# The second block of a two-model kernel in another order, with VectorE and ScalarE in written order

## The chip, the cores and the metric

The kernel runs on one core of a Trainium2 chip. The metric is device time in microseconds (us), the median of several executions. Before the change it is 2164.07 us, the median of 3 runs from 2163.93 to 2165.48. The engines are TensorE (PE; its weight loads are PEld), VectorE (DVE), ScalarE (ACT), GpSimd (POOL) and SyncE (SP), which issues the loads of weights.

## The reference, cut to what matters

256 tokens of width 1024 in float32 go through a first model (two layers, each with a mixer and a product-key expert stage) and then through a second block. The change lies in the mixer half of the second block:

```python
def second_block(x, ...):
    h = rmsnorm(x, ln1_g)                    # x: the first model's normed output
    z = h @ w_in                             # 1024 -> pool 256, mLSTM q,k 512, v 256, o 256, i,f 8, attention q,k,v 1536
    po = pool_mixer(z[pool], pool_w, pool_scale)
    qk = silu(causal_dwconv(z[mq,mk], m_conv))         # 4 taps
    mo = sigmoid(z[o]); mi, mf = z[i] + b_i, z[f] + b_f
    hm = mlstm(qk, z[v], mi, mf)                       # log-sigmoid, cumulative sum, running maximum
    hm = rmsnorm(hm, m_norm_g) * mo
    aq, ak = rmsnorm(z[q], a_q_g), rmsnorm(z[k], a_k_g)   # per head, 8 heads of 64
    ao = moba_attention(aq, ak, z[av])                 # causal softmax within the 256 tokens
    x = x + concat([po, hm, ao]) @ w_out
    ...                                                # norm, gated FF with a 3-tap conv, unchanged
```

Two norms meet at its start: the first model's last norm (gain `gbc`) gives the residual stream, and `ln1` the input of `w_in`. The kernel computes both scales at once from x and from y = x * gbc.

## The kernel before, in words

**Units of weights.** All matrices stream from memory once, in pieces of 128 x 1024 float32 (512 KB) that are called units; `units` fixes their order, and SP loads them in that order, up to four ahead. Each unit is split into two reduced-precision parts, so that three products give float32 accuracy: ScalarE rounds the raw unit into `wh` (line 127) and VectorE or GpSimd subtracts it for `wl` (line 128, by the letters of `lo_on["pat"]`). There are four raw buffers and three of `wh` and `wl`; `prepare()` issues the split of the unit three ahead, so the high part waits until TensorE has done the unit just used.

**Two kinds of products.** `c_unit` (lines 159 to 161) gives 128 channels by 256 tokens: 24 matmuls of 256 columns into one bank. `t_mm` (lines 177 to 181) takes the activations as columns of 512: 12 matmuls into banks 4 to 7, which stay occupied over all units of a token-major product. The eight PSUM banks are called `bank_92` to `bank_99` in the built program, that is banks 0 to 7.

**Start of the block.** The expert stage ends in banks 4 to 7. `landing` adds these to x (line 245 in the last stage) and transposes x by 128 x 128 into banks 0 to 3; `settle` turns the transposes into `xh` (ScalarE, line 278) and `xl` (VectorE, line 279), 16 of each. `norm_scales_final` takes sums of squares on ScalarE and makes two inverse roots with one Newton step each; `spread` makes two diagonal matrices in `gt` (line 328) and lets TensorE spread the scale over all partitions into `rbc`, by which the channel-major results are multiplied.

**The 31 units of `block2`.** In this order: 8 token-major units `tm` (mLSTM v and o, attention v), one unit for the gates (`gw`), 4 for the mLSTM's q and k (`mqk`), 8 for the attention's q and k (`aqk`), 2 for pooling (`pin`), and 8 of the output product (`wo`). Between them stand `gates` (32 rows by 256 tokens, with Abs, Exp and Ln on ScalarE and two scans on VectorE), `conv4` (four taps on VectorE and a Silu each), `ml_*` (the mLSTM), and `at_*` (attention by pairs of heads: normalise, scores, softmax, transpose, values).

**What sets the order.** TensorE's and SP's instructions stand in the order in which they are written. VectorE's, ScalarE's and GpSimd's are ordered by a scheduler, and `behind()` and `keep_in_program_order` hold single ones back. In the block, low parts go to GpSimd from the gates to the fourth output unit (`lo_on["pat"] = "P"`), and by a pattern before.

Of the kernel before, what the change touches and what calls it, by code (L numbers as in the profile page):

```python
# [40 lines left out]
def kernel(ctx: ExitStack, tc: tile.TileContext, a, out):  # L41
# [43 lines left out]

    units = []
    for nm in a["order"]:
        w = a[nm]
        units += [w[i] for i in range(w.shape[0])]
# [82 lines left out]
    def t_mm(h, l, sh, sl, first, last):  # L172
        for b in range(2):
            bs = slice(b * 128, b * 128 + 128)
# [97 lines left out]
    def settle(g, low=False, dst=None):  # L272

        h, l = dst or (xh, xl)
        for b in range(2):
# [26 lines left out]
    def norm_scales_final(gbc):  # L302


        y = ar(120, 8).rearrange("p (b d) -> p b d", b=2)
        q = 32
        for b in range(2):
            for n in range(2):
                ns = slice(n * 512, n * 512 + 512)
                P.tensor_tensor(y[:, b, ns], x[:, b, ns], gbc[:, ns], op=ALU.mult)  # L310
                with behind(st["after"]):
                    sumsq(b, n)
                    sumsq(b, n, y, q)
            V.tensor_scalar(col(b, 2), col(b, 0), 1.0 / 1024, EPS, op0=ALU.mult, op1=ALU.add)
            V.tensor_scalar(col(b, 7), col(b, 0, q), 1.0 / 1024, None, op0=ALU.mult)
            V.tensor_scalar(col(b, 4), col(b, 1), 1.0 / 1024, col(b, 2), op0=ALU.mult, op1=ALU.add)
            V.tensor_scalar(col(b, 2, q), col(b, 4), EPS, col(b, 7), op0=ALU.mult, op1=ALU.add)
            S.activation(col(b, 3, q), col(b, 1, q), AF.Sqrt, bias=col(b, 2, q), scale=1.0 / 1024)
            V.tensor_scalar(col(b, 4, q), col(b, 1, q), 1.0 / 1024, col(b, 2, q), op0=ALU.mult, op1=ALU.add)
            root(b, q)  # L320
            S.activation(col(b, 3), col(b, 4), AF.Sqrt)
            root(b)
            V.tensor_scalar(x[:, b], y[:, b], col(b, 5), None, op0=ALU.mult)

    def spread(bk, off=0):

        for b in range(2):
            V.tensor_scalar(gt[b][:, :128], ident, col(b, 5, off), None, op0=ALU.mult)
            T.matmul(bk[:, b * 128:b * 128 + 128], ones, gt[b][:, :128], start=True, stop=True)
        V.tensor_copy(rbc, bk[:, :256])  # L330
# [19 lines left out]
    V.tensor_tensor(sm[:, 48:56], cols[:, C_FNG:C_FNG + 8], cols[:, C_LN1:C_LN1 + 8], op=ALU.mult)  # L350

# [483 lines left out]
    def block2():  # L835
        sg = ar(64, 2).rearrange("p (b n) -> p b n", b=2)
        settle(g2, low=True)

        for k in range(8):
            h, l = unit()  # L840
            t_mm(h, l, xh[:, k], xl[:, k], k == 0, k == 7)
            prepare()
            if k == 0:
                norm_scales_final(gbc)
        for b in range(2):
            r = col(b, 5, 32)
            S.activation(vau[:, b, :, 0:64], bank[4 + b * 2][:, 0:256].rearrange("p (h e) -> p h e", h=4),
                         AF.Copy, scale=r)
            S.activation(sg[:, b], bank[4 + b * 2][:, 256:512], AF.Sigmoid, scale=r)
            S.activation(tok[:, b, 512:1024], bank[5 + b * 2], AF.Copy, scale=r)  # L850
        spread(bank[3], 32)
        V.memset(vau[:, :, :, 64:65], 1.0)
        table("natural_log_exp_and_others")
# [8 lines left out]
        V.memset(onz, 1.0)  # L862

        def gates():
            V.tensor_tensor(g64, bank[2][0:64, :256], rbc[0:64], op=ALU.mult)
            V.tensor_scalar(g64, g64, cols[0:64, C_MBI:C_MBI + 1], None, op0=ALU.add)
            f = g64[32:64]
            S.activation(lf[:, 0], f, AF.Abs)
            S.activation(lf[:, 0], lf[:, 0], AF.Exp, scale=-1.0)
            V.tensor_scalar(lf[:, 1], lf[:, 0], 1.0, None, op0=ALU.add)  # L870
            S.activation(lf[:, 2], lf[:, 1], AF.Ln)
            V.tensor_scalar(lf[:, 3], lf[:, 1], -1.0, None, op0=ALU.add)
            V.tensor_tensor(lf[:, 0], lf[:, 0], lf[:, 3], op=ALU.subtract)
            last = S.activation(lf[:, 1], lf[:, 2], AF.Exp, scale=-1.0)
            V.tensor_tensor(lf[:, 0], lf[:, 0], lf[:, 1], op=ALU.mult)
            V.tensor_tensor(lf[:, 0], lf[:, 0], lf[:, 2], op=ALU.add)
            V.tensor_scalar(lf[:, 1], f, 0.0, None, op0=ALU.min)
            V.tensor_tensor(gc, lf[:, 1], lf[:, 0], op=ALU.subtract)
            V.tensor_tensor_scan(gc, onz[0:32], gc, 0.0, op0=ALU.mult, op1=ALU.add)
            V.tensor_tensor(R[0:32], g64[0:32], gc, op=ALU.subtract)  # L880
            V.tensor_tensor_scan(mx, onz[0:32], R[0:32], 0.0, op0=ALU.mult, op1=ALU.max)
# [462 lines left out]
```

## Time and profile before

| | |
|---|---|
| median of 3 runs | 2164.07 us |
| profiled execution, its own time | 2165.04 us |
| its span / mean granted TensorE clock | 2162.9 us / 0.994 |
| TensorE busy | 2123.0 us (98%) |
| VectorE / ScalarE / GpSimd busy | 1598.8 / 1141.7 / 223.4 us |
| second block's mixer half on TensorE | from 1830.28 to about 1965.5 us |

Busy times are of one execution. A matmul's end is modelled, so a busy TensorE is not TensorE at its peak; the granted clock (PEclk) tells how fast its clock was, with 1.00 for 2.4 GHz and 0.50 for 1.2 GHz. Idle time counts where the engine that bounds the stretch waits.

### The profile page before, as it was taken

Reading aid. Unit: us, or ns where it says so; the run is one execution under the profiler, and the core shown is the slowest. Engines: PE = TensorE matmul, PEld = TensorE weight load, DVE = VectorE, ACT = ScalarE, POOL = GpSimd, SP = SyncE. Lnnn points to the kernel's source line nnn. Section 1 sums busy time; section 2 is a strip of 40 time slices with the busy share of each in tenths; the row PEclk is TensorE's granted clock in tenths of the full one; section 3 lists DMA queues with packets and bytes.
Section 4 is the critical chain, followed back from the end, with each engine's and each line's share of the span. In section 5 each row is a group of like instructions: output and inputs, shape, how many; then the busy total and the mean of one; then the engine's idle time right before and its main releaser. Section 6 shows DMA issues by size and latency. Waiting matters only on the chain.

```text
span 2162.9 us, 38249 instructions
## 1 busy us (share of the span) xinstructions
PE 2123.0 (98%) x14590; PEld 1938.0 (90%) x14590; DVE 1598.8 (74%) x3167; ACT 1141.7 (53%) x2096; POOL 223.4 (10%) x106
## 2 busy tenths in 40 slices
PE   9999999999999999999999999999999999889999
PEld 8899999999988888887999999998888887778998
DVE  7779878896566666675788788965666666797997
ACT  5454545555555555566545555545555555655443
POOL 0008000000000000052170000000000001550000
PEclk9999999999999999999999999999999999999999
DMA  7586654555667666633556555556676665434654
GB/s 231 175 243 196 187 166 156 157 157 169 207 198 232 208 194 194 185 118 111 178 180 186 163 154 155 155 176 209 193 221 194 193 195 166 146 98 145 187 185 146
DMA packets 109024, 384.44 MB, mean 178 GB/s; under 512 B 11876, under 2 KB 15332, under 8 KB 108584
## 3 DMA queue, kind: packets, MB, share of 16 engines
q1 hardware_dynamic: 108552, 381.81, 57.1%
q8 instruction: 114, 1.87, 0.4%
q14 instruction: 70, 0.57, 0.1%
q10 hardware_dynamic: 288, 0.19, 0.0%
HBM read 374.61 MB, written 7.34 MB: 177 GB/s over the span
## 4 chain that ended last, share of the span: by engine, by line
PE 92%; DVE 4%; ACT 2%; issue 1%; DMA 1%; POOL 0%; SPq 0%; ACTq 0%; POOLq 0%
PE bank L159 16%; PE bank L160 16%; PE bank L161 16%; PE bank L177 12%; PE bank L178 12%; PE bank L181 12%; PE bank L560 3%; ACT wh L127 1%; PE bank L429 1%; DVE arena L898 1%; DVE arena L765 0%; DVE wl L128 0%; DVE x L243 0%; DMA x<-in_x_dram 0%; PE bank L782 0%
## 5 line engine op out<-in xcount | busy, mean ns | idle before, releaser
L127 ACT ACTIVATE wh<-raw 128x1024 fp32r<-128x1024 f32 x691 | 732.5, 1060 | 497.4 <-PE bank L160 292.4
L128 DVE TENSOR_TENSOR wl<-raw,wh 128x1024 fp32r<-128x1024 f32 x607 | 744.8, 1227 | 299.8 <-ACT wh L127 298.7
L159 PE MATMUL bank<-xh,wh 128*128 128x256 f32 x2792 | 805.6, 289 | 7.3 <-ACT arena L900 4.9
L161 PE MATMUL bank<-xh,wl 128*128 128x256 f32 x2792 | 791.7, 284 | 0.9 <-POOL wl L138 0.9
L160 PE MATMUL bank<-xl,wh 128*128 128x256 f32 x2792 | 791.9, 284 | 0.0
L159 PEld LDWEIGHTS bank<-xh,wh 128*128 128x128 f32 x2792 | 537.0, 192 | 12.4 <-ACT arena L900 5.1
L160 PEld LDWEIGHTS bank<-xl,wh 128*128 128x128 f32 x2792 | 537.4, 192 | 1.5 <-DVE xl L279 0.8
L161 PEld LDWEIGHTS bank<-xh,wl 128*128 128x128 f32 x2792 | 536.9, 192 | 1.8 <-POOL wl L138 1.7
L177 PE MATMUL bank<-wh,ah 128*128 128x512 f32 x1160 | 454.2, 392 | 3.3 <-ACT arena L775 3.3
L178 PE MATMUL bank<-wl,ah 128*128 128x512 f32 x1160 | 453.1, 391 | 0.0
L181 PE MATMUL bank<-wh,al 128*128 128x512 f32 x1160 | 358.7, 390 | 0.0
L128 POOL TENSOR_TENSOR wl<-raw,wh 128x1024 fp32r<-128x1024 f32 x84 | 204.7, 2439 | 1048.0 <-ACT wh L127 1042.8
L177 PEld LDWEIGHTS bank<-wh,ah 128*128 128x128 f32 x1160 | 218.6, 188 | 50.4 <-ACT arena L775 4.2
L181 PEld LDWEIGHTS bank<-wh,al 128*128 128x128 f32 x1160 | 218.9, 189 | 45.9
L186 ACT ACTIVATE ah<-arena 128x256 fp32r<-128x256 f32 x270 | 112.1, 416 | 279.5 <-PE bank L178 278.0
L178 PEld LDWEIGHTS bank<-wl,ah 128*128 128x128 f32 x1160 | 218.7, 189 | 44.4
L187 DVE TENSOR_TENSOR al<-arena,ah 128x256 fp32r<-128x256 f32 x270 | 114.6, 426 | 122.2 <-PE bank L181 110.9
L551 DVE TENSOR_TENSOR x<-iota,ijT 128x1024 f16<-128x1024 f16 x128 | 88.5, 693 | 52.2 <-PE bank L560 52.2
L574 ACT ACTIVATE arena<-bank 128x276 f32<-128x276 f32 (+42 forms) x128 | 37.9, 296 | 131.5 <-DVE arena L572 131.5
L553 DVE TENSOR_TENSOR x<-x,wT 128x1024 f16<-128x1024 f16 x128 | 87.6, 685 | 0.0
L560 PE MATMUL bank<-x 128*128 128x128 f16 x1024 | 81.2, 220 | 0.0
L310 POOL TENSOR_TENSOR top<-x,arena 128x512 f32<-128x512 f32 x4 | 5.1, 1290 | 693.1 <-DVE x L245 693.1
(302 smaller groups left out, 1841.7 us busy)
## 6 DMA issues: line engine op xcount, KB each, us to landing
raw<-in_u_dram SPq DMA_DIRECT2D x256, 512.0 KB, 3.5
raw<-in_v_dram SPq DMA_DIRECT2D x256, 512.0 KB, 3.6
raw<-in_ff_dram SPq DMA_DIRECT2D x66, 512.0 KB, 3.5
raw<-in_wq_dram SPq DMA_DIRECT2D x32, 512.0 KB, 3.6
raw<-in_conv_in_dram SPq DMA_DIRECT2D x23, 512.0 KB, 3.8
raw<-in_conv_out_dram SPq DMA_DIRECT2D x8, 512.0 KB, 3.5
f_d<-arena SPq DMA_DIRECT2D x8, 512.0 KB, 7.2
raw<-in_aq_dram SPq DMA_DIRECT2D x8, 512.0 KB, 3.9
```

The costliest lines, as they stand in the source:

```text
L127: S.activation(h, r, AF.Copy)
L128: (P if pat[lo_on["i"] % len(pat)] == "P" else V).tensor_sub(l, r, h)
L159: T.matmul(out_ps, hv[:, k], ah[:, k], start=k == 0, stop=False)
L160: T.matmul(out_ps, hv[:, k], al[:, k], start=False, stop=False)
L161: T.matmul(out_ps, lv[:, k], ah[:, k], start=False, stop=k == 7)
L177: T.matmul(bank[4 + b * 2 + n], sh[:, bs], h[:, ns], start=first, stop=False)
L178: T.matmul(bank[4 + b * 2 + n], sh[:, bs], l[:, ns], start=False, stop=False)
L181: T.matmul(bank[4 + b * 2 + n], sl[:, bs], h[:, ns], start=False, stop=last)
L186: S.activation(h, src, AF.Copy)
L187: V.tensor_sub(l, src, h)
L551: V.tensor_tensor(E, iota[:, None, None, :, :].to_broadcast(shape), ijT[:, c, :, :, None, :].to_broadcast(shape), op=ALU.is_equal)
L560: T.matmul(bk[:, t * 128:t * 128 + 128], E[:, 0, t // 2, :, t % 2], W[:, q, t // 2, :, t % 2], start=q == 0, stop=q == 1)
```

## The change

The units are loaded and used in another order: gates, pooling 2, `mqk` 4, `aqk` 0 to 3, then `tm` 0 to 7 amid the first two attention pairs, then `aqk` 4 to 7 and the output units by `WO_ROWS`. Inside the block VectorE and ScalarE too now follow the written order (`manual_schedule`), and every low part is VectorE's (21 of them were GpSimd's). The norm is written in pieces: y on GpSimd, sums of squares of y on VectorE, roots one unit later, diagonals before the fourth unit, `spread` after it. The gates come in four parts, one per unit; the first tap of each convolution goes to ScalarE. The attention's norm takes Ln, Exp and Square on ScalarE straight from the bank; its maxima are taken in the pass that adds the mask (`tensor_tensor_reduce`). Results that were copied into `mix` are split straight from the bank. The sigmoid of the o gate is taken late, in `sg_out`, between two table loads of ScalarE. At the end of the diff the new sequence is condensed to a line per unit, with the unit's number behind it.

```diff
+WO_ROWS = [0, 3, 6, 7, 1, 2, 4, 5]
...
+            for part, lo, hi in (("gw", 0, 1), ("pin", 0, 2), ("mqk", 0, 4), ("aqk", 0, 4), ("tm", 0, 8), ("aqk", 4, 8)):
+                units += [a[part][i] for i in range(lo, hi)]
...
-    def settle(g, low=False, dst=None):
+    def settle(g, low=False, dst=None, maker="P"):
...
-                pat, lo_on["pat"] = lo_on["pat"], "P"
+                pat, lo_on["pat"] = lo_on["pat"], maker
                 pump_split(st["use"] + 2)
...
-    def norm_scales_final(gbc):
+    def norm_y(gbc, y):
+    ...
+    def norm_scales_final(b, y, z, q=32):
+        for n in range(2):
+            ns = slice(n * 512, n * 512 + 512)
+            sumsq(b, n)
+            V.tensor_tensor_reduce(z, y[:, b, ns], y[:, b, ns], 1.0, 0.0, op0=ALU.mult, op1=ALU.add,
+                                   accum_out=col(b, n, q))
+    ...
+        S.activation(col(b, 3, q), col(b, 1, q), AF.Sqrt, bias=col(b, 2, q), scale=1.0 / 1024)
+    ...
+        S.activation(col(b, 3), col(b, 4), AF.Sqrt)
+    def norm_roots_final(b, q=32):
+        root(b, q)
+        root(b)
...
     def block2():
-        settle(g2, low=True)
-        for k in range(8):
-            ...
-                norm_scales_final(gbc)
+        lo_on["pat"] = "V"
+        norm_y(gbc, y)
+        settle(g2, low=True, maker="V")
+        order = ExitStack()
+        order.enter_context(tc.manual_schedule(engines={mybir.EngineType.DVE, mybir.EngineType.Activation}))
...
+        def sg_out():
+            for b in range(2):
+                S.activation(sg[:, b], bank[4 + b * 2][:, 256:512], AF.Sigmoid, scale=col(b, 5, 32))
+            S.preload_act_table_set("natural_log_exp_and_others")
...
-        def at_n(c):
-            T.matmul(bank[2], bones, z2[c % 2], start=True, stop=True)
-            V.tensor_scalar(zs, bank[2], 1.0 / 64, EPS, op0=ALU.mult, op1=ALU.add)
-            rsqrt_small(z, zs, zt)
+        def at_n(c, bk):
+            T.matmul(bk, bones, z2[c % 2], start=True, stop=True)
+            S.activation(z2[c % 2], bk, AF.Ln, bias=sm[:, 58:59], scale=1.0 / 64)
+            S.activation(z2[c % 2], z2[c % 2], AF.Exp, scale=-0.5)
+            S.activation(zt, z2[c % 2], AF.Square, scale=0.125)
+        def at_q(c, bk):
+            ...
...
-            V.tensor_reduce(mx3, L.rearrange("p h (s n) -> p h s n", s=3), axis=AX.X, op=ALU.max)
+                    V.tensor_tensor_reduce(L[:, h, ls], bank[banks[h]][:, ls], cm[:, ls], -1.0, 1e30,
+                                           op0=ALU.add, op1=ALU.min, accum_out=nm[:, h, b:b + 1])
...
-            V.tensor_copy(mix[4 + c], o[:, 0:256])
...
+        some_unit(bank[2]); prepare(); norm_scales_final(0, y, zt)                            # unit 1
+        some_unit(bank[0]); prepare(); norm_roots_final(0); norm_scales_final(1, y, zt)       # 2
+        some_unit(bank[1]); prepare(); norm_roots_final(1); diagonal(32)                      # 3
+        some_unit(bank[3]); prepare(); spread(bank[7], 32, True)                              # 4
+        some_unit(bank[4]); gates(0); pool_in(0), pool_in(1); prepare(); ...; conv_u(0, bank[3])   # 5
+        some_unit(bank[5]); prepare(); gates(1); conv_u(1, bank[4]); conv_t(0); ...x by y...  # 6
+        some_unit(bank[6]); prepare(); gates(2); conv_u(2, bank[5]); conv_t(1)                # 7
+        at_u(0, 0); prepare(); gates(3); conv_u(3, bank[6]); conv_t(2)                        # 8
+        at_u(0, 1); prepare(); conv_t(3); ...Silu x4...; T.transpose(bank[3], R); ...         # 9
+        at_u(1, 0); ...ml_d...  at_u(1, 1); ...                                               # 10, 11
+        tm_unit(0) ... tm_unit(7), with at_n, at_q, at_b, at_b2, at_c of pairs 0 and 1        # 12 to 19
+        at_u(2, 0); tm_out(); ...ml_v...                                                      # 20
+        at_u(2, 1); ...; at_z(2); ml_fin(0); sg_out()                                         # 21
+        at_u(3, 0); prepare(); at_n(2, bank[2]); ml_fin(1)                                    # 22
+        at_u(3, 1); prepare(); at_q(2, bank[2]); fetch(mix[0]); at_z(3)                       # 23
+        wo(0); prepare(); at_b(2, (0, 3)); at_n(3, bank[2]); ml_fin(2)                        # 24
+        wo(1) ... wo(5), with ml_out and the rest of pairs 2 and 3                            # 25 to 29
+        order.close()
```

The first place is TensorE at the start of the block: the last transposes of x into banks 0 to 3 (`bank_92` to `bank_95`), then the first unit. Before, that unit is token-major:

```order
L269 MATMUL bank_92<-ident,x 128x128 x2
L269 MATMUL bank_93<-ident,x 128x128 x2
L269 MATMUL bank_94<-ident,x 128x128 x2
L269 MATMUL bank_95<-ident,x 128x128 x2
L177 MATMUL bank_96<-wh,xh 128x512
L178 MATMUL bank_96<-wl,xh 128x512
L177 MATMUL bank_97<-wh,xh 128x512
L178 MATMUL bank_97<-wl,xh 128x512
```

Now the gates' unit stands there, into bank 2 (`bank_94`):

```order
L280 MATMUL bank_92<-ident,x 128x128 x2
L280 MATMUL bank_93<-ident,x 128x128 x2
L280 MATMUL bank_94<-ident,x 128x128 x2
L280 MATMUL bank_95<-ident,x 128x128 x2
L168 MATMUL bank_94<-xh,wh 128x256
L169 MATMUL bank_94<-xl,wh 128x256
L170 MATMUL bank_94<-xh,wl 128x256
```

The first unit moved from banks that the transposes do not use to one that they do.

The second place is VectorE in the norm (`sm` holds its columns of sums and roots). Before, the small operations of both token blocks stand next to each other:

```order
L319 TENSOR_SCALAR sm<-sm 128x1
L252 RECIPROCAL sm<-sm 128x1 x2
L253 TENSOR_SCALAR sm<-sm 128x1 x2
L254 TENSOR_SCALAR sm<-sm 128x1
L314 TENSOR_SCALAR sm<-sm 128x1
L254 TENSOR_SCALAR sm<-sm 128x1
L290 TENSOR_SCALAR sm<-sm 128x1 x2
L323 TENSOR_SCALAR x<-top,sm 128x1024
L328 TENSOR_SCALAR gt_84<-ident,sm 128x128
L128 TENSOR_TENSOR wl<-raw,wh 128x1024
```

Now the sums of squares of y (L325) precede them, and a unit's low part (L137) stands between the sums and the roots of one block:

```order
L325 ISA arena,sm<-top 128x512
L325 ISA sm 128x1
L327 TENSOR_SCALAR sm<-sm 128x1
L328 TENSOR_SCALAR sm<-sm 128x1
L329 TENSOR_SCALAR sm<-sm 128x1
L330 TENSOR_SCALAR sm<-sm 128x1
L332 TENSOR_SCALAR sm<-sm 128x1
L137 TENSOR_TENSOR wl<-raw,wh 128x1024
L263 RECIPROCAL sm<-sm 128x1
L264 TENSOR_SCALAR sm<-sm 128x1
L265 TENSOR_SCALAR sm<-sm 128x1
L301 TENSOR_SCALAR sm<-sm 128x1
```

What moved is the low part: the roots' Newton steps are queued behind it.

The third place is ScalarE at the sigmoid (`bank_96` and `bank_98` hold the o gate). Before, it stands right behind the token-major units:

```order
L847 ACTIVATE arena<-bank_96,sm 128x4x64
L849 ACT_TABLE_LOAD
L849 ACTIVATE arena<-bank_96,sm 128x256
L850 ACTIVATE arena<-bank_97,sm 128x512
L847 ACTIVATE arena<-bank_98,sm 128x4x64
L849 ACTIVATE arena<-bank_98,sm 128x256
L127 ACTIVATE wh<-raw 128x1024
L850 ACTIVATE arena<-bank_99,sm 128x512
L257 ACT_TABLE_LOAD
```

Now it stands between the mLSTM's denominators (L967, L969) and the high part (L136) of a later unit:

```order
L1013 ACTIVATE arena<-arena 128x512
L967 ACTIVATE arena<-arena 128x8
L969 ACTIVATE arena<-bank_97 128x4
L969 ACTIVATE arena<-bank_99 128x4
L881 ACT_TABLE_LOAD
L881 ACTIVATE arena<-bank_96,sm 128x256
L881 ACTIVATE arena<-bank_98,sm 128x256
L882 ACT_TABLE_LOAD
L136 ACTIVATE wh<-raw 128x1024
```

The two table loads moved with it, into the stretch of the third attention pair's norm.

## Rows read from the trace of the kernel before

**Rows 1.** Page part 1, whole span: engine, busy time (share of span) and instructions.

```profile
PE 2123.0 (98%) x14590; PEld 1938.0 (90%) x14590; DVE 1598.8 (74%) x3167; ACT 1141.7 (53%) x2096; POOL 223.4 (10%) x106
```

**Rows 2.** Windows of core 0: from:to, length, five engines' busy (x), PEclk, DMA, GB/s.

```profile
1620.00:1700.00 80.00, 80.00 (x355) 66.26 (x354) 48.52 (x60) 43.48 (x60) 0.00 (x0) 1.00 0.64 195
1860.00:1880.00 20.00, 13.92 (x93) 13.21 (x92) 18.79 (x27) 9.08 (x13) 11.02 (x5) 0.83 0.44 132
1900.00:1920.00 20.00, 19.22 (x156) 17.04 (x156) 19.71 (x42) 11.54 (x32) 9.43 (x4) 1.00 0.33 107
1920.00:1940.00 20.00, 14.48 (x79) 10.68 (x78) 19.26 (x41) 8.69 (x20) 8.65 (x7) 0.83 0.26 79
```

**Rows 3.** TensorE's waits, 1830 to 1966: us in total, times, longest.

```profile
PE bank L159 <- ACT arena L900: 4.9, 1, 4.9
PE bank L1026 <- DVE arena L1019: 2.8, 1, 2.8
PE bank L1001 <- DVE arena L987: 2.7, 2, 2.1
PE bank L1063 <- ACT arena L1064: 1.8, 1, 1.8
PE bank L981 <- ACT arena L978: 1.4, 1, 1.4
PE bank L178 <- POOL wl L128: 0.9, 1, 0.9
PE bank L1093 <- DVE arena L882: 0.8, 1, 0.8
PE bank L1026 <- DVE arena L983: 0.8, 1, 0.8
...
```

**Rows 4.** Windows of single stretches of TensorE; columns as in rows 2.

```profile
1871.40:1876.80 5.40, 5.40 (x24) 5.15 (x24) 5.37 (x9) 0.90 (x1) 2.46 (x1) 0.50 0.24 61
1896.40:1899.30 2.90, 2.90 (x24) 2.90 (x25) 2.90 (x3) 0.80 (x2) 2.66 (x1) 1.00 0.21 85
1928.50:1933.00 4.50, 4.50 (x27) 4.37 (x25) 3.94 (x10) 1.92 (x4) 0.00 (x0) 0.62 0.00 0
```

**Rows 5.** Timeline at the block's start: start, us, instruction, [idle before <-releaser].

```profile
1830.06 4.40 DVE L279 SCALAR_TENSOR_TENSOR xl<-bank,sm,xh 128x128 fp32r<-128x128 f32 x16 [0.25 <-ACT xh L278]
...
1830.28 0.47 PE L177 MATMUL bank<-wh,xh 128*128 128x512 f32 x1
```

**Rows 6.** Timeline, 1864 to 1870, VectorE and GpSimd; columns as in rows 5.

```profile
1864.06 4.88 POOL L128 TENSOR_TENSOR wl<-raw,wh 128x1024 fp32r<-128x1024 f32 x2 [1.76 <-ACT wh L127]
1864.10 2.66 DVE L898 SCALAR_TENSOR_TENSOR arena<-arena,cols 128x256 f32<-128x256 f32 x1
...
1866.79 2.44 DVE L875 TENSOR_TENSOR arena<-arena 32x256 f32<-32x256 f32 x1
```

**Rows 7.** Groups by form, several stretches: instruction xcount | busy us, mean ns | idle before.

```profile
L128 DVE TENSOR_TENSOR wl<-raw,wh 128x1024 fp32r<-128x1024 f32 x30 | 36.8, 1226 | 18.0 <-ACT wh L127 18.0
...
L127 ACT ACTIVATE wh<-raw 128x1024 fp32r<-128x1024 f32 x30 | 31.9, 1062 | 1.1
...
L749 DVE CUSTOM_DVE_ANT_0 arena<-bank,arena 128x256 f32<-128x256 f32 x32 | 14.0, 477 | 1.8 <-PE bank L740 1.8
...
L1181 DVE SCALAR_TENSOR_TENSOR arena<-arena,cols 128x256 f32<-128x256 f32 x44 | 21.2, 483 | 0.5
...
L186 ACT ACTIVATE ah<-arena 128x256 fp32r<-128x256 f32 x270 | 112.1, 416 | 279.5 <-PE bank L178 278.0 <-DVE arena L1036 1.2 <-DVE arena L1184 0.3
...
L257 ACT ACT_TABLE_LOAD x3 | 3.8, 1283 | 0.1
...
L337 DVE SCALAR_TENSOR_TENSOR arena<-arena 128x512 f32<-128x512 f32 x4 | 2.7, 686 | 0.0
...
L318 ACT ACTIVATE sm<-sm 128x1 f32<-128x1 f32 x2 | 0.6, 287 | 0.0
L254 DVE TENSOR_SCALAR sm<-sm 128x1 f32<-128x1 f32 x4 | 0.6, 146 | 0.0
```

More of the change, by code (lines that the diff above doesn't have):

```diff
@@ L86 @@
     units = []
+    second = ("tm", "gw", "mqk", "aqk", "pin")
     for nm in a["order"]:
         w = a[nm]
-        units += [w[i] for i in range(w.shape[0])]
+        if nm == "tm":
+            for part, lo, hi in (("gw", 0, 1), ("pin", 0, 2), ("mqk", 0, 4), ("aqk", 0, 4), ("tm", 0, 8), ("aqk", 4, 8)):
+                assert hi <= a[part].shape[0]
+                units += [a[part][i] for i in range(lo, hi)]
+        elif nm not in second:
+            units += [w[i] for i in (WO_ROWS if nm == "wo" else range(w.shape[0]))]
     st = {"dma": 0, "split": 0, "use": 0, "after": None}
@@ L170, in t_half, with t_mm @@
         T.matmul(o, sl[:, bs], h[:, ns], start=False, stop=last)
-    def t_mm(h, l, sh, sl, first, last):
+    def t_mm(h, l, sh, sl, first, last, between=None):
         for b in range(2):
+            if b and between:
+                between()
             bs = slice(b * 128, b * 128 + 128)
@@ L862, in block2, with gates @@
         V.memset(onz, 1.0)
-        def gates():
-            V.tensor_tensor(g64, bank[2][0:64, :256], rbc[0:64], op=ALU.mult)
-            V.tensor_scalar(g64, g64, cols[0:64, C_MBI:C_MBI + 1], None, op0=ALU.add)
+        V.memset(vau[:, :, :, 64:65], 1.0)
+        def gates(k):
             f = g64[32:64]
[L868 to L881, printed above, removed]
-            V.tensor_tensor(R[32:64], gc, mx, op=ALU.add)
-            return last
@@ L955, in ml_out @@
+        def ml_out(bk):
+            bk = bk.rearrange("p (c t) -> p c t", c=2)
             for b in range(2):
@@ L1083, in block2 @@
-        c_unit(bank[2][:, :256])
-        ml_unit(0)
-        last = gates()
-        ml_unit(1)
-        conv4(0, last)
-        ml_unit(2)
-        conv4(1, last)
-        ml_unit(3)
-        conv4(2, last)
+            t_mm(h, l, sh, sl, k == 0, False, between)
+        some_unit(bank[2])
+        prepare()
+        norm_scales_final(0, y, zt)
+        some_unit(bank[0])
+        prepare()
+        norm_roots_final(0)
+        norm_scales_final(1, y, zt)
+        some_unit(bank[1])
+        prepare()
@@ new lines, in block2 @@
+        norm_roots_final(1)
+        diagonal(32)
+        some_unit(bank[3])
+        prepare()
+        spread(bank[7], 32, True)
+        some_unit(bank[4])
+        gates(0)
+        for i in range(2):
+            pool_in(i)
+        prepare()
+        S.preload_act_table_set("natural_log_exp_and_others")
+        conv_u(0, bank[3])
+        some_unit(bank[5])
+        prepare()
+        gates(1)
+        conv_u(1, bank[4])
+        conv_t(0)
+        for b in range(2):
+            V.tensor_scalar(x[:, b], y[:, b], col(b, 5), None, op0=ALU.mult)
@@ L1092, in block2 @@
+        some_unit(bank[6])
+        prepare()
+        gates(2)
+        conv_u(2, bank[5])
+        conv_t(1)
+        at_u(0, 0)
+        prepare()
+        gates(3)
+        conv_u(3, bank[6])
+        conv_t(2)
+        at_u(0, 1)
+        prepare()
+        conv_t(3)
+        for i in range(4):
+            S.activation(qk[i], yc4[i], AF.Silu)
+        S.preload_act_table_set("natural_log_exp_and_others")
         for b in range(2):
@@ L1113, in block2 @@
-        ml_s(2)
-        ml_s(3)
-        at_u(2, 1)
-        at_z(2)
-        at_b2(0)
+        pool_work()
+        tm_unit(0)
+        prepare()
+        at_n(0, bank[0])
+        ml_s(0, bank[2])
+        ml_s(1, bank[3])
+        tm_unit(1)
+        prepare()
+        at_q(0, bank[0])
+        at_n(1, bank[1])
+        tm_unit(2)
+        prepare()
+        ml_s(2, bank[2])
+        ml_s(3, bank[3])
+        at_q(1, bank[1])
+        tm_unit(3)
+        prepare()
+        at_b(0, (0, 2))
+        tm_unit(4)
@@ L1158, in block2 @@
-        wo(5)
-        fetch(7)
+        wo(0)
+        prepare()
+        at_b(2, (0, 3))
+        at_n(3, bank[2])
+        ml_fin(2)
+        wo(1)
+        prepare()
+        ml_out(bank[1])
+        fetch(mix[1])
+        at_b2(2)
+        fetch(bank[1][:, 0:256])
+        wo(2)
+        prepare()
+        fetch(bank[1][:, 256:512])
+        at_q(3, bank[2])
+        wo(3)
+        prepare()
+        at_c(2, (0, 3))
+        at_b(3, (1, 2))
+        wo(4)
+        prepare()
+        at_d(2, bank[0])
```

283 lines of the change are left out of this document (144 added, 139 removed).

## The prediction

> **What bounds the kernel now.** The page first: TensorE is busy 98% of the span [rows 1], so nothing outside a stretch where it waits can move the time much. The table by stage then shows where that is: in the expert stage TensorE is busy for all of 80 us at full clock, while in the second block, 1860 to 1880 and 1920 to 1940, it is busy 13.9 and 14.5 of 20 us at a mean granted clock of 0.83, with VectorE at 18.8 and 19.3 of 20 [rows 2]. The list of waits of TensorE in the block names eight that sum to 16.1 us, the longest 4.9 us for a Silu of ScalarE that itself stood behind VectorE's taps, then 2.8 us and 2.7 us for VectorE [rows 3]. After the first the granted clock is 0.50 for a whole unit: 24 matmuls take 5.40 us where 2.90 us is the full-speed time; 27 later matmuls take 4.50 us at 0.62, where 27/24 of 2.90 would be 3.26 [rows 4]. With under 1 us for the ten transposes before those, the slow clock costs 2.5 + 1.2 + 0.8 = 4.5 us. Everything the block can gain on TensorE is so 16.1 + 4.5 = 20.6 us, about 1%. The matmuls themselves are the same ones before and after.
>
> **What the change takes away.** It moves 21 low parts from GpSimd to VectorE. Rows show why that is no plain load: while GpSimd ran two low parts in 4.88 us, a tap of 0.48 us took 2.66 us on VectorE and a 32-row operation 2.44 us, each ending as a low part ended [rows 6, 7]. I count the 20.6 us as gone, all of them, and then ask what is late next. The new load, 21 x 1.23 = 25.8 us [rows 7], lies beside TensorE as long as a slot (one unit of weights) has room: 2.90 us for a channel-major unit, 12 x 80.00/355 = 2.7 us for a token-major one [rows 2, 4].
>
> **What it adds: written order.** In each slot ScalarE's high part waits for the end of the unit just multiplied (three buffers), VectorE's low part waits for that, and all later work of the slot now stands behind them. So a slot's VectorE work begins at the earliest 1.06 us after a unit's end [rows 7]. I add durations along these waits; an operation that needs nothing from the one before starts about 0.08 us before that one's end (the 16 rows of 0.34 us in 4.40 us), a dependent one 0.03 us after it. Units are numbered 1 to 31 in the new order.
>
> 1. Start. Unit 1 now writes bank 2, where the transposes of x have landed, so it waits for the settling to have read that bank: for the 15th of the 16 low parts of xh. They ran from 1830.06 to 1834.46 beside TensorE, whose first unit began at 1830.28 in banks 4 to 7 [rows 5]. One weights' low part (1.23 us) now also stands before the last add of x. 15 x 0.275 from 1830.9, with 0.3 for ScalarE's alternation, gives 1835.3: a wait of 5.0 us, and unit 1 at 0.50 of the clock, 2.5 us more [rows 4].
> 2. Norm to spread. From the end of unit 1: high part 1.06, low part 1.15, two sums of squares on VectorE 1.5, four small operations 0.75, two square roots 0.45; then unit 5's high part queued behind the roots 1.06, its low part 1.15, eight small operations of the two Newton steps 1.7 (0.15 to 0.29 each [rows 7]); block 1 the same, 1.5 + 0.75 + 0.45 + 1.06 + 1.15 + 1.7; two diagonals 0.5. Sum 15.9 us. The spread's matmuls stand behind unit 4 only: three units, 8.7 us. Wait 7.2 us. The 512-wide sum of squares has no row: it lies between the 256-wide fused one, 0.48 + 0.08, and twice that; I take 0.75, by the 0.69 of a 512-wide operation [rows 7]. The ends move this step by -0.7 and +1.2.
> 3. Gates to transpose. From the diagonals to the last gate operation, which the transpose ahead of unit 10 needs: 2.95 (low part, rbc, gate and pool inputs) is hidden, because unit 5, slow again, ends at 5.85 (spread 0.4, unit 5.45); high part 1.06, low part and first conv input 1.5, high part of the next 1.5 (behind ScalarE's first tap), low part 1.15 to 11.1; then one busy queue: gates 1.3, conv input 0.35, three taps 1.43 (0.48 each [rows 7]), the two scalings of x 1.4; low part, gates 2, input, taps 4.8; low part and gates 3 2.7. Sum 23.1 us, against 0.4 + 5 x 2.90 = 14.9 us of TensorE. Loss 8.2 us, of which some 2.5 is slow clock. Behind it unit 10 runs at 0.50: 2.5 us.
> 4. Token-major part. Slots hold 2.1 to 4.2 us of VectorE work against 3.6 to 4.8 us on TensorE (2.7 and a piece of attention): hidden, as the change means. One chain is not: the first softmax's four exponentials (0.42 us each and their gaps, 1.75 us [rows 7]) stand ahead of a high part on ScalarE, whose low part stands ahead of the four scalings: 1.8 us.
> 5. Pair 2. From the end of unit 21: the two head outputs and their split 2.2, low part and the normalised input on VectorE to 3.6, the square and three small ones on ScalarE to 4.6, then two table loads of 1.28 us [rows 7] around two sigmoids, 3.4, a high part 1.06, a low part 1.15, the mLSTM norm's two 512-wide operations 1.65, two small ones and unit 26's high part 1.5, low part 1.15, four operations of at_q 2.2. Sum 16.8 us; TensorE has 11.2 us in it (units 22 to 24 at 2.9, 2.9 and 2.7, head outputs 1.7, norm 1.0). Wait 5.6 us.
> 6. To the end of the block: slow clock after that wait 2.3, the mLSTM output 0.8, scores of pair 3 0.9, its transposes 0.9, and the last high split, which stands behind the table load for Sqrt, 1.2 us. Together 6.1 us.
>
> ScalarE's table load is the term for which a page has another price: "ScalarE: Activation LUTs" of the Trainium skill (section on what the load costs) gives about 2.7 us, where rows 7 show 1.283 us for each. By the page's figure step 5 would be 2.8 us longer and step 6 1.4 us; the trace has the duration, so it stays out.
>
> Edits at no cost: the copies of mix that fall away and the maxima now fused into one pass shorten VectorE inside slots that are hidden or counted above; without that cover the copies (256 wide, so about one tap's 0.48 us each) would only make step 6 shorter. The SP queue issues the same loads in another order, four ahead, with the DMA engines busy 0.26 to 0.44 in these stretches [rows 2]; if a load came late, each would cost at most its lag once.
>
> **Sum.** 5.0 + 2.5 + 7.2 + 8.2 + 2.5 + 1.8 + 5.6 + 6.1 = 38.9 us lost after, 20.6 us lost before: 18.3 us more. The profiled execution took 2165.04 us, 0.97 us over the median of the runs: 2164.07 + 18.3 = 2182.4, and I say 2182.
>
> **Rivals.** A: faster. The exclusion of VectorE and GpSimd is what made the old waits, and with it gone the new queues keep up. For it: three lines alone, 12 taps, 8 products and others, show single operations of five times their length, as in rows 6, and VectorE is full where TensorE waits [rows 2]. Against it: step 2 needs its 15.9 us to shrink under 8.7 us and step 3 its 23.1 under 14.9, with no operation in them that GpSimd ever lengthened. If they do and step 5 too, 5.0 + 2.5 + 1.8 and half of step 6 remain, 12.4 us against 20.6: 2156 us. It decides from the point where both norms finish within three units. Chance 0.18: the sums of steps 2 and 3 rest on waits between engines that no row of before shows in this order. "SBUF — State Buffer" of the Trainium skill (its entry on the shared port pair) says VectorE and GpSimd hold it exclusively, the loser fully blocked; by that rule alone the block would take this course, and the trace agrees on the blocking: 2.66 us for a tap of 0.48.
> B: no change. The scheduler's overlaps are about half hidden: if steps 2, 3, 5 and 6 (27.1 us) come to a third of that, the sum is 11.8 + 9.0 = 20.8 against 20.6, 2164 us. It would need ScalarE's high parts to run ahead of their place, which written order forbids. Chance 0.06.
> C: worse. The slow clock reaches further than the one unit seen: behind four waits of 5 to 8 us, another 2.5 us each, 10 us: 2192 us. The 0.62 of the second stretch speaks for less [rows 4]. Chance 0.12.
> That the change does not do what it says is excluded: the built order shows it on all engines.
>
> **How the numbers follow.** The forecast, 10 to 26 us slower, has 0.64. Within 0.2%, 4.3 us, is what a measurement cannot tell from no change. Faster by more: A, 0.18. Same: B, 0.06. Slower by more: the forecast and C, 0.76. The range, 2160 to 2193, leaves out the larger part of A and the far end of C. The forecast's own is 2174 to 2190: the bounds of the sums of squares, and a fifth of the 18 us.
>
> **What would show it.** Right: TensorE's waits name xl (about 5 us at the block's start), gt (about 7), a gate's arena tile before a transpose (about 6), at_q's arena tile after the first output unit (5 to 6); granted clock 0.50 behind each; GpSimd idle but for the pooling. VectorE's taps all near 0.48 us show only that the exclusion went. Wrong: if gt comes before unit 4 ends, or the transposes' wait is under 2 us, steps 2 and 3 fall and A is near.

## The result, and the profile after

The changed kernel takes 2181.61 us (2179.84 to 2184.55, 4 runs) against 2164.0 us (2163.84 to 2165.48, 4 runs), a ratio of 1.0082 with a 95% interval of 1.0066 to 1.0098: 17.6 us slower, where 18.3 were worked out. The profiled execution took 2184.55 us, 19.5 more than that of before. A block is measured here from the first of the last stage's transposes of x to the first transpose behind its output units. These are the two windows, before and after (columns as in [rows 2]):

```profile
1825.23:1965.49 140.26, 123.20 (x735) 102.47 (x735) 111.53 (x215) 80.80 (x159) 65.82 (x34) 0.94 0.38 117
```

```profile
1828.14:1985.38 157.24, 126.59 (x735) 105.40 (x735) 99.75 (x227) 82.75 (x163) 14.66 (x13) 0.91 0.34 107
```

The same 735 matmuls take 17.0 us longer: TensorE is idle for 30.7 us instead of 17.1 (+13.6) and busy for 3.4 us more, since more of them ran at half clock. VectorE has 21 more low parts (25.8 us by [rows 7]) and yet 11.8 us less busy time, and GpSimd is almost idle. The spans of the two profiles differ by 19.9 us (2182.8 and 2162.9). The other 2.9 us lie ahead of the block, where both kernels issue the same work (the program's first 100 us had a granted clock of 0.97 after, 1.00 before), and behind it nothing differs; I count the block alone.

The waits of TensorE in the block (engine line <- what it waited for: us in total, times, longest), which answer to [rows 3]:

```profile
PE bank L1043 <- DVE arena L1030: 7.0, 2, 5.5
PE bank L348 <- DVE gt L341: 6.6, 1, 6.6
PE bank L1174 <- DVE arena L916: 6.2, 1, 6.2
PE bank L168 <- DVE xl L290: 3.5, 1, 3.5
PE bank L1069 <- DVE arena L1062: 1.5, 2, 0.8
PE bank L1104 <- ACT arena L1105: 1.5, 1, 1.5
PE bank L280 <- DVE x L256: 1.4, 2, 1.1
PE bank L177 <- ACT ah L197: 1.2, 1, 1.2
```

Four of the eight old entries are gone (4.9 us for the Silu, 1.4, 0.9 and one of 0.8). The other four pairs are still here under new line numbers: the softmax's transposes (2.8 before, 1.5 now), the scores (2.7 and 7.0), the pooling (1.8 and 1.5) and the gates' transposes (0.8 and 6.2). The four long entries are the four that the prediction named: xl at the start, gt at the spread, the last gate operation, at_q (5.5 of the 7.0 us). The stretches behind the waits for xl, gt and the last gate operation, as windows:

```profile
1838.00:1843.30 5.30, 5.30 (x25) 5.30 (x26) 1.58 (x2) 1.01 (x2) 0.00 (x0) 0.50 0.32 99
1859.60:1864.90 5.30, 5.30 (x31) 5.30 (x31) 2.26 (x6) 2.51 (x4) 0.00 (x0) 0.60 0.41 113
1882.60:1888.00 5.40, 5.40 (x27) 5.14 (x26) 4.90 (x10) 4.79 (x8) 0.00 (x0) 0.53 0.43 152
```

The units in them take 5.3, 4.8 and 5.2 us where [rows 4] have 2.90; the granted clock falls to or near the lower of its two levels, 1.2 GHz, after each long idle time (behind the fourth, from 1954.87 to 1960, it is 0.56). VectorE is busy for only 1.6 and 2.3 us in the first two, and for 4.9 us in the third.

The taps of the convolutions, 1855 to 1895, before and after (group | busy us, mean ns | idle before):

```profile
L898 DVE SCALAR_TENSOR_TENSOR arena<-arena,cols 128x256 f32<-128x256 f32 x12 | 13.9, 1156 | 0.3
```

```profile
L933 DVE SCALAR_TENSOR_TENSOR arena<-arena,cols 128x256 f32<-128x256 f32 x12 | 5.8, 482 | 0.3
```

So the exclusion of [rows 6] did go, and 8.1 us of VectorE with it on these twelve alone. It was no longer what TensorE waited for.

What sets the time between the spread and the gates is seen in ScalarE's timeline there (start, length, instruction, [idle before <- releaser]; lines left out are marked):

```profile
1867.19 0.51 ACT L928 ACTIVATE arena<-arena,cols 128x256 f32<-128x256 f32 x1 [0.33 <-DVE arena L926]
1867.60 1.04 ACT L136 ACTIVATE wh<-raw 128x1024 fp32r<-128x1024 f32 x1
...
1871.75 0.51 ACT L928 ACTIVATE arena<-arena,cols 128x256 f32<-128x256 f32 x1 [1.08 <-DVE arena L926]
1872.16 1.05 ACT L136 ACTIVATE wh<-raw 128x1024 fp32r<-128x1024 f32 x1
1873.23 0.42 ACT L908 ACTIVATE arena<-arena 32x256 f32<-32x256 f32 x1
1878.09 0.51 ACT L928 ACTIVATE arena<-arena,cols 128x256 f32<-128x256 f32 x1 [4.44 <-DVE arena L926]
1878.50 1.04 ACT L136 ACTIVATE wh<-raw 128x1024 fp32r<-128x1024 f32 x1
1882.78 0.51 ACT L928 ACTIVATE arena<-arena,cols 128x256 f32<-128x256 f32 x1 [3.23 <-DVE arena L926]
```

and in VectorE's:

```profile
1865.59 1.23 DVE L137 TENSOR_TENSOR wl<-raw,wh 128x1024 fp32r<-128x1024 f32 x1 [3.66 <-ACT wh L136]
...
1868.68 1.23 DVE L137 TENSOR_TENSOR wl<-raw,wh 128x1024 fp32r<-128x1024 f32 x1 [1.52 <-ACT wh L136]
...
1874.39 1.22 DVE L137 TENSOR_TENSOR wl<-raw,wh 128x1024 fp32r<-128x1024 f32 x1
...
1877.67 0.39 DVE L926 TENSOR_TENSOR arena<-bank,rbc 128x256 f32<-128x256 f32 x1
1877.98 1.50 DVE L933 SCALAR_TENSOR_TENSOR arena<-arena,cols 128x256 f32<-128x256 f32 x3
1879.58 1.23 DVE L137 TENSOR_TENSOR wl<-raw,wh 128x1024 fp32r<-128x1024 f32 x1
...
1881.87 0.42 DVE L916 TENSOR_TENSOR arena<-arena 32x256 f32<-32x256 f32 x1
```

There are two parts. Up to 1868.7 VectorE waits for ScalarE's high parts: 3.66 us behind the slow unit, then 1.52 us, because that high part (L136) stands behind the first tap of a convolution (L928) and the tap behind VectorE's conv input (L926). From there on VectorE is the busy queue, 13.0 of the 13.7 us up to 1882.3, and it is ScalarE that waits, 4.44 us before a tap: gates, conv inputs, taps and low parts (L137) follow each other on VectorE without a gap. The last gate operation (L916) ends at 1882.3, 23.4 us after the diagonals.

### The profile page after: what moved, and what is told of

It reads as the page before. It is cut to its first block, busy times and chain, and to the rows that moved or that the text cites. A ratio compares the mean times of both kernels' runs of the same rounds, so it can differ in the third digit from the quotient of the medians.

```text
span 2182.8 us, 38240 instructions
## 1 busy us (share of the span) xinstructions
PE 2129.6 (98%) x14590; PEld 1943.9 (89%) x14590; DVE 1588.5 (73%) x3183; ACT 1143.6 (52%) x2100; POOL 172.3 (8%) x85
## 4 chain that ended last, share of the span: by engine, by line
PE 92%; DVE 4%; ACT 2%; issue 1%; DMA 1%; SPq 0%; ACTq 0%; DVEq 0%
PE bank L168 17%; PE bank L169 16%; PE bank L170 16%; PE bank L188 12%; PE bank L192 12%; PE bank L189 12%; PE bank L583 3%; ACT wh L136 1%; DVE wl L137 1%; PE bank L452 1%; DVE arena L788 0%; DMA x<-in_x_dram 0%; DVE x L254 0%; PE bank L805 0%; PE bank L177 0%
## 5 line engine op out<-in xcount | busy, mean ns | idle before, releaser
L137 DVE TENSOR_TENSOR wl<-raw,wh 128x1024 fp32r<-128x1024 f32 x628 | 769.0, 1225 | 342.8 <-ACT wh L136 340.7
L136 ACT ACTIVATE wh<-raw 128x1024 fp32r<-128x1024 f32 x691 | 732.3, 1060 | 497.1 <-PE bank L169 294.0
L137 POOL TENSOR_TENSOR wl<-raw,wh 128x1024 fp32r<-128x1024 f32 x63 | 152.9, 2428 | 1055.5 <-ACT wh L136 1051.4
L168 PE MATMUL bank<-top,wh 128*128 128x256 f32 x256 | 76.3, 298 | 0.3
```

Source lines behind the costliest of these rows:

```text
L136: S.activation(h, r, AF.Copy)
L137: (P if pat[lo_on["i"] % len(pat)] == "P" else V).tensor_sub(l, r, h)
L168: T.matmul(out_ps, hv[:, k], ah[:, k], start=k == 0, stop=False)
```

## The experiments

Each was run beside the kernel before on the same chip. The block is measured as above, on each run's profile; "waits" are TensorE's.

| run | median, before beside it (us) | ratio, 95% interval | block (us) |
|---|---|---|---|
| before / after | 2164.0 / 2181.61 | 1.0082 (1.0066 to 1.0098) | 140.3 / 157.2 |
| e1_sched | 2184.93, 2166.31 | 1.0084 (1.0068 to 1.0101) | 151.5 |
| e2_low_pool | 2176.63, 2166.31 | 1.0043 (1.0026 to 1.0060) | 153.1 |
| e3_before_V | 2161.86, 2166.31 | 0.9981 (0.9971 to 0.9990) | 137.3 |
| e4_sigmoid | 2180.87, 2166.31 | 1.0062 (1.0045 to 1.0078) | 153.8 |
| e5_diag | 2181.44, 2166.24 | 1.0070 (1.0053 to 1.0087) | 156.1 |
| e6_late_tr | 2184.61, 2166.24 | 1.0085 (1.0068 to 1.0101) | 159.7 |
| e7_fill | 2181.24, 2166.24 | 1.0073 (1.0056 to 1.0090) | 155.6 |
| e9_V_late | 2158.82, 2166.24 | 0.9963 (0.9951 to 0.9976) | 135.0 |
| e10_ml_first | 2162.12, 2166.18 | 0.9984 (0.9975 to 0.9994) | 136.8 |
| e11_copy_first | 2182.19, 2166.18 | 1.0070 (1.0053 to 1.0087) | 158.6 |
| e12_gates_first | 2186.86, 2165.27 | 1.0100 (1.0085 to 1.0115) | 162.2 |
| e13_scores_late | 2160.91, 2165.27 | 0.9978 (0.9969 to 0.9987) | 136.3 |

**e1, the new units under the scheduler.**

```diff
-        order.enter_context(tc.manual_schedule(engines={mybir.EngineType.DVE, mybir.EngineType.Activation}))
```

> The changed kernel with its new order of units and all low parts on VectorE, but with VectorE and ScalarE left to the scheduler in the block (the line with manual_schedule is gone). Theory (the waits come from the written order's chains, slot by slot): in this program the norm's sums and roots stand ahead of and amid the settling, so the wait for the diagonals (6.65 us) falls under 2 us, the first unit's wait for xl (3.5 us) grows to 6 to 9 us because some 5 us of norm work stand before it, and the wait before the gates' transposes (6.25 us) falls by 2 us or more: 2170 to 2178 us. Rival (the order of units and VectorE's load make the loss, whoever sorts the queues): 2179 us or more, with VectorE busy through the waits.

Its long waits in the block (line numbers are one lower there):

```profile
PE bank L1173 <- DVE arena L915: 9.7, 1, 9.7
PE bank L168 <- DVE xl L290: 7.3, 1, 7.3
PE bank L1042 <- DVE arena L1029: 3.8, 1, 3.8
```

The wait for the diagonals went and that for xl doubled, as expected; the wait for the gates grew from 6.25 to 9.7 us instead of falling. The block is 5.8 us shorter than in written order and 11.2 longer than before. The median is no better, because the scheduler also sorted VectorE anew at the program's start: up to the block TensorE waits 12.6 us for diagonals there, 6.6 in the changed kernel. The time and the rival's other sign came out as the rival said: over 2179 us, with VectorE busy through the two longest waits (9.0 of 9.7 us and all of 7.3). By the block, written order costs some 6 us, and two thirds of the loss are there without it.

**e2, low parts back on GpSimd** (25 of them).

```diff
-        lo_on["pat"] = "V"
+        lo_on["pat"] = "P"       # and maker="P"; "V" again behind wo(0)
```

> The changed kernel with the low parts of the block back on GpSimd up to the first output unit (25 of them, 4 more than before the change), all else as written. Theory (chains in written order): each small operation of the norm no longer stands behind a low part of 1.15 us, so the chain from the first unit to the diagonals shortens by two or three of them, 6.65 us of wait become 3.5 to 5; but two engines share the block again, taps take over 1 us on the mean, and the later waits stay or grow: 2176 to 2188 us. Rival (the 21 low parts moved to VectorE are the cost): at least half of the 17.6 us comes back, 2173 us or less.

The time is in the theory's range, the terms are only in part: the wait for gt is 5.8 us in two, more than the 3.5 to 5 expected; the gates' wait is 6.3 as before; taps take 0.85 us on the mean, not over 1; the wait of pair 2 fell to 3.6 us instead of staying. The block is 4.2 us shorter. In this written order a low part on VectorE costs more than the exclusion does; whether by its place or by its length was not separated.

**e3, the kernel before with only its low parts moved.**

```diff
-        settle(g2, low=True)
+        lo_on["pat"] = "V"
+        settle(g2, low=True, maker="V")
...
-        lo_on["pat"] = "P"
         c_unit(bank[2][:, :256])
```

> The kernel before with nothing but every low part of the block on VectorE, its scheduler and its order of units kept. Theory (VectorE has room for them as long as the queue is sorted by need; the exclusion goes): taps fall to 0.48 us, the waits for the Silu (4.9 us) and for the products behind VectorE shrink or move, 2158 to 2167 us. Rival (the load of 25.8 us more on VectorE is what made the change slower): 2173 us or more.

The theory's side: 4.5 us faster than before, block 3.0 us shorter, taps at 0.480 us. The wait for the Silu (4.9 us) went, and 5.7 us came before the gates' transposes, so that TensorE's idle time in the block fell only from 17.1 to 16.3 us. VectorE's busy time there fell from 111.5 to 107.2 us, with 21 low parts more on it. So under the old order the 25.8 us of VectorE work make no loss.

**e4, the sigmoids one unit earlier.**

```diff
         tm_out()
         prepare()
+        sg_out()
...
         ml_fin(0)
-        sg_out()
```

> The changed kernel with the two sigmoids and their two table loads one unit earlier, behind the high part of unit 20, where ScalarE is idle most of the time. Theory (they stand in the chain of the third attention pair): the wait before that pair's scores, 5.5 us, falls by 3.4 us to about 2.1, and the time by 3 to 6 us (a shorter wait may also spare the slow unit behind it): 2176 to 2179 us. Rival (VectorE's low parts and the norm of the mLSTM hold the chain, the sigmoids run beside): the wait stays within 1 us of 5.5 and the time within 1.5 us of 2181.6.

```profile
1952.04 0.50 PE L1043 MATMUL bank<-arena 64*128 64x128 f32 x4 [2.20 <-DVE arena L1030]
```

The wait went from 5.51 to 2.20 us and the block from 157.2 to 153.8, by 3.4 us: the two table loads and two sigmoids stood in that chain with their full length. The median, 2180.87 us, missed the 2176 to 2179 expected; set against the kernel before beside it, which took 2.3 us longer this time, it is 14.6 us slower instead of 17.6.

**e5, the spread without the norm.**

```diff
-            V.tensor_scalar(gt[b][:, :128], ident, col(b, 5, off), None, op0=ALU.mult)
+            V.tensor_scalar(gt[b][:, :128], ident, sm[:, 59:60] if off else col(b, 5, off), None, op0=ALU.mult)
...  # diagonal(32) behind unit 1
```

> The changed kernel with the first norm scale left out of the spread: the diagonals are made from a constant (0.02) right behind the first unit, all sums, roots and Newton steps still run where they stood. Its output is not the model's. Theory (VectorE's written queue is the bound from 1838 to 1882, the wait for gt is only where TensorE notices it): the spread no longer waits (6.65 us to under 1), but the gates still stand behind the norm's last root on VectorE, so TensorE waits 12 us or more before the gates' transposes instead of 6.25, and the block gets shorter by 0 to 3 us. Rival (the terms are independent, as my sum added them): 6.65 us and a slow unit of 2.4 us go, the block is 9 us shorter.

The spread did not wait, the gates' transposes waited 8.20 us (12 or more were expected), later units waited for high and low parts (3.7 us in four waits), and the block was 1.1 us shorter. The wait for gt is where TensorE notices the queue, not its price.

**e6, the gates' transposes two units later, and e11, the same with the copy ahead of its slot's parts and the early sigmoids.**

```diff
-        for b in range(2): T.transpose(bank[3]..., R...); V.tensor_copy(bt, ...)      # behind unit 9
+        ...                                                                           # behind unit 11, ml_d one slot later
```

> The changed kernel with the transposes of the gates and the copy behind them two units later (behind unit 11), the mLSTM's decays one slot later. Theory (TensorE came early to a fixed chain): two units of 2.9 us pass first, the wait of 6.25 us falls to under 1.5 and the slow unit behind it (2.4 us) is spared: block 6 to 8.6 us shorter. Rival (the low parts of the next units stand behind the same queue): units 11 and 12 wait for wl instead, and the block is within 2 us of 157.2.

> The changed kernel with the transposes of the gates behind unit 11 as in the run before, but with their copy ahead of that slot's high and low part in the written order, and with the sigmoids one unit earlier. Theory (in written order the copy stood behind two low parts that waited for ScalarE's Silus; what counts is the place in the queue): the wait of 8.06 us for the copy falls under 3, and with the 3.4 us of the sigmoids the block comes to 147 to 151 us. Rival (the gates' chain itself is late, or the next low parts take the wait over): the first 60 us of the block do not get shorter than in the changed kernel, and the block stays at 153.8, as with the sigmoids alone, or above.

Neither brought the theory's gain (159.7 and 158.6 us); e6 is even longer than its rival's range. The transposes no longer wait, but what needs their copy does, 8.1 us in e6. In e11:

```profile
1890.06 1.22 PE L940 MATMUL bank<-arena 4*128 4x256 f32 x2 [6.92 <-DVE arena L1181]
```

The copy (L1181) still stands behind the low part of the slot ahead, that behind a high part, and that behind ScalarE's four Silus between two table loads (1882.5 to 1887.0 in that run).

**e7, idle matmuls in two waits.**

```diff
+        for _ in range(24):
+            T.matmul(bank[6][:, 0:128], ones, ones, start=True, stop=True)
         spread(bank[7], 32, True)
...  # and 22 into bank[7] ahead of the gates' transposes
```

> The changed kernel with idle matmuls of a matrix of ones in two of the waits (24 before the spread, 22 before the gates' transposes, 5 to 5.5 us each at full clock), into banks that are free. Theory (a wait of TensorE costs twice, by its length and by a unit at half clock behind it): units 5 and 10 take 2.9 us at a granted clock near 1.0 instead of 5.3 us at 0.50, block 4.8 us shorter. Rival (the slow unit has another reason, or the filling delays what follows): within 1 us of 157.2, or longer.

The clock part held; the windows behind the two waits:

```profile
1855.24:1861.00 5.76, 5.76 (x48) 5.76 (x49) 3.05 (x8) 3.21 (x5) 0.00 (x0) 1.00 0.48 159
1877.70:1883.00 5.30, 4.66 (x32) 4.18 (x33) 5.05 (x10) 4.41 (x8) 0.00 (x0) 1.00 0.41 129
```

But the block gained 1.6 us, not 4.8: a unit that ends earlier only meets the next chain earlier. The second wait, filled part included, is 7.6 us (5.1 filled, 2.5 left) where it was 6.25.

**e9 and e13, the kernel before, improved.** e9 is e3 with the gates' transposes behind `at_u(0, 1)`; e13 is e9 with `at_b(0, (3, 4))` behind `at_u(2, 1)`.

> The kernel before with all low parts of the block on VectorE, and the transposes of the gates two units later. Theory: the wait of 5.65 us before these transposes, the longest that the run with all low parts on VectorE showed, goes with the slow unit behind it; block 129 to 133 us (137.3 there, 140.3 before the change), 8 us or more under the kernel before. Rival (what was waited for there is waited for behind: the decays and scores of the mLSTM need the same copy): block within 1.5 us of 137.3.

> The kernel before with all low parts on VectorE and the gates' transposes two units later (135.0 us of block), and with the scores of the first attention pair behind one more unit. Theory (the longest wait left, 4.79 us, is for that pair's norm on VectorE, and a unit of 2.9 us can pass before it): wait 1.9 us or less, block 130 to 133 us, some 9 us under the kernel before. Rival (the softmax behind it becomes late by as much): block within 1 us of 135.0.

e9 is the fastest of all, 7.4 us under the kernel before beside it (ratio 0.9963, 0.9951 to 0.9976). Its block, 135.0, is 2.3 us under e3's, less than the 4 to 8 expected: the wait of 5.7 us went and one of 4.8 came before the first pair's scores. e13 lost that one, and one of 5.0 us came for the mLSTM's scores behind it, one of 3.6 us before later scores: block 136.3. Both theories missed their range.

**e10, e3 with the gates and mLSTM units ahead of the token-major ones**, spread behind the fourth unit (condensed):

```diff
-        tm 0-7 (norm behind tm 0); spread(bank[3], 32); gw; mqk 0-3; T.transpose R
+        gw (norm behind it); mqk 0-2; spread(bank[7], 32); gates(); mqk 3; tm 0-7; T.transpose R
```

> The kernel before with all low parts of the block on VectorE (137.3 us of block), where only the units are put in another order: gates and the four mLSTM units first, with the spread behind the fourth, then the eight token-major units. Scheduler, norm, gates and attention as in the kernel before. Theory (the token-major units need no scale, and were the cover of settling, norm and gates): the first unit waits some 3.5 us for xl and runs at half clock (2.4 us), and the diagonals, 14.5 us behind the settling in the run with the old order, meet a spread 14 us behind it, so 0 to 3 us more; the gates are covered by the token-major units now: block 143 to 148 us. Rival (the place of the token-major units matters little, the new block is slow by its rewritten parts): within 2 us of 137.3.

My theory fell: 136.8 us. The first unit waits 3.5 us for xl, as expected, but nothing waits for gt, and the gates' wait of 5.7 us is gone, since eight token-major units now lie beside them (last gate operation 17.8 us after `rbc` begins to be copied; 22.3 in the changed kernel). Putting the gates and the mLSTM's units first is not the loss.

**e12, the gates ahead of the taps in the written queue.**

```diff
         gates(2)
-        conv_u(2, bank[5])
-        conv_t(1)
+        conv_t(0)
+        conv_u(2, bank[5])
...  # the same with gates(3); x by y to tm 1; the copy of the gates ahead of its slot's parts
```

> The changed kernel, same units, only the written order of VectorE in four slots: each part of the gates ahead of the convolution taps, taps one slot later, the two scalings of x (1.4 us) moved from the sixth slot to a token-major one, the copy of the gates ahead of its slot's high and low part. Theory (a place in the written queue sets when the gates end, not VectorE's load, which stays the same): the last gate operation comes 4 to 6 us earlier against the spread, the wait of 6.25 us before the gates' transposes falls under 2.5, and the block is 3 to 7 us shorter than 157.2. Rival (the queue only hands the wait on, as with the later transposes): the Silus come later by what the gates gain, the next units wait for their high and low parts, and the block stays within 2 us of 157.2.

Worse than both: 162.2 us, the gates' wait 6.68. The last gate operation came no earlier: it ends 22.4 us after `rbc` begins to be copied, 22.3 in the changed kernel, and the 5 us were lost behind the transposes. ScalarE's rows show why the gates gained nothing:

```profile
1876.47 0.51 ACT L928 ACTIVATE arena<-arena,cols 128x256 f32<-128x256 f32 x1 [4.86 <-DVE arena L926]
1876.88 1.04 ACT L136 ACTIVATE wh<-raw 128x1024 fp32r<-128x1024 f32 x1
...
1882.71 0.51 ACT L928 ACTIVATE arena<-arena,cols 128x256 f32<-128x256 f32 x1 [4.79 <-DVE arena L926]
1883.13 1.04 ACT L136 ACTIVATE wh<-raw 128x1024 fp32r<-128x1024 f32 x1
```

and VectorE's:

```profile
1871.20 1.23 DVE L137 TENSOR_TENSOR wl<-raw,wh 128x1024 fp32r<-128x1024 f32 x1 [1.52 <-ACT wh L136]
...
1877.95 1.23 DVE L137 TENSOR_TENSOR wl<-raw,wh 128x1024 fp32r<-128x1024 f32 x1 [1.52 <-ACT wh L136]
```

I had put taps ahead of `conv_u` on VectorE, so the conv input came later, with it the first tap on ScalarE, behind that the high part, and VectorE's next low part waited 1.52 us for it, twice, where it had not waited before. Here the two engines did take turns: a place on one engine's queue moved the other's. Taking the first taps off ScalarE's queue was not tried.

## Why the prediction was right, point by point

- **What goes.** I counted all the old waits as gone, by the exclusion. That was too much: e3 takes only the exclusion away and leaves 16.3 of 17.1 us of idle time, and four of the eight pairs wait in the changed kernel too. The sum holds all the same, because it sets every wait after against every wait before. TensorE's idle time before was 17.1 us by the block's window, 16.1 in my list.
- **Step 1, start.** The first unit begins 9.85 us after the block's first transposes, 5.05 before the change: 4.8 us, worked out 5.0, and the unit took 5.3 us. The wait for xl itself is 3.5 us of that, less than the 5 named; the last transposes' wait for x, 1.1 us where there was none before, is another part. The reason was loose: a channel-major unit reads both token blocks of `xh` and `xl` from its first matmul on, and in the order of `settle` the second block begins with the ninth of the 16 low parts, so another bank alone would have freed the unit only in part. e10 waits the same 3.5 us with the same bank, and no run had a free bank there.
- **Step 2, norm to spread.** Unit 1 ends at 1843.3, the spread starts at 1858.75: 15.4 us against 15.9; wait 6.65 against 7.2. The 512-wide sum of squares took 0.69 us and 0.08 for reading its sum, where I took 0.75.
- **Step 3, gates.** From the diagonals to the last gate operation 23.4 us against 23.1; wait 6.25 us against 5.7, and a slow unit in it and one behind it, as said. The rows also bear out how the sum was put together: waits for high parts first, then one busy queue on VectorE.
- **Step 4.** Waits of 1.1, 0.75 and 1.5 us amid the attention pairs against 1.8 in one: 1.5 too little.
- **Step 5, pair 2.** 16.6 us from the end of unit 21 (1938.24) to the scores (1954.87) against 16.8; wait 5.5 against 5.6. e4 moved it by the 3.4 us that stood for the sigmoids. The trace's 1.283 us for a table load was the right duration: seven loads in the block have that mean, and what stands behind these two on ScalarE begins 0.02 us after them.
- **Step 6.** Waits of 0.6, 1.5, 0.8 and 1.2 us against 0.8, 0.9, 0.9 and 1.2.
- **The sum.** Waits grew by 13.6 us, by the steps by 13; slow clock by some 3.4, by the steps 5.3. The size missed is the clock's, and e7 shows that its price is not a term of its own where a chain of other engines follows: removing two slow units, some 2 us longer each than at full clock, gave 1.6.
- **The reason was too simple in one place.** I put the loss down to written order, and e1 has two thirds of it without. By blocks, from one profile each, e3 shows the move of the low parts at -3.0 us, e10 the place of the token-major units at -0.5, and the step from e1 to the changed kernel written order at +5.8. The remaining 14.7, between e10 and e1, hold four attention units ahead of the token-major ones (so that the gates meet their reader five units behind the spread, not nine), y's sums on VectorE amid the settling, first taps on ScalarE, the split gates and the other rewritten parts. Which of these it is was not separated. VectorE is busy through the long waits of e1 and through most of that before the gates' transposes in the changed kernel, which speaks for too much VectorE work between the spread and the gates' reader, but no run shows that alone.
- **Rivals.** A needed the norm and gates to keep up; neither did. (That GpSimd had never lengthened an operation of these two steps was wrong: the 32-row operation of [rows 6] is one of the gates. With GpSimd idle the steps took their 15.4 and 23.4 us all the same.) B's third did not happen. C's longer slow clock did not show: one unit behind each wait. The move of low parts cost 4.2 us in the changed kernel (e2) and paid 3.0 us in the one before (e3), so rival A's mechanism is real, though not in this order. The two kernels differ in more than their queues, so that the queues make this difference is argued, not shown.

## What to carry to other kernels

Work out a hand-written order as a chain through all engines, slot by slot, with the shared instructions (here the splitting of weights) in it: an engine can set the time while it is busy for 35.3 of 52 us, as VectorE from 1838 to 1890. A wait removed alone is often only handed on (e5, e6, e7, e11, e13), so look at what stands next in that queue first. Of a change with many parts, try the part with its own reason alone: low parts on VectorE under the old order, with one transpose moved, were 0.37% faster than before.

## What the runs showed of the hardware that was not expected

Idle matmuls of ones kept the granted clock at 1.00 through waits of 6.65 and 6.25 us, of which 1.4 and 2.5 were left unfilled (48 records of 128 columns in 5.52 us), and the units behind ran at full speed; that was expected in e7, but not that only 1.6 of 4.8 us would come back. Low parts on GpSimd could hold far smaller work than taps: in e2 the two 128x128 diagonals took 4.16 us together, beside two low parts of 4.64 us, where they took 0.47 with GpSimd idle.
